# A two-layer mixer block: one projection moved ahead of the recurrence's end, four turns before its inverse, tails by banks, attention turns

## The chip, the core and the metric

The kernel runs on one core of one Trainium2 chip. The time is the device time of one execution in microseconds (us); of several executions the median is given.

## The reference

Two layers of three sublayers on x (256 rows by 1024): a gated feed-forward (width 2816), a mixer and a second feed-forward, each with an RMS norm ahead of it and one behind it. All is fp32.

```python
x = x + 0.5 * rms(ffn1(rms(x, pre)), post)
x = x + rms(mixer(rms(x, pre)), post)
x = x + 0.5 * rms(ffn2(rms(x, pre)), post)

def mixer(h):
    z_dsa, z_rwkv, z_diff, z_gate = split(h @ w_in)
    y_a = top-k attention (4 heads of 128, index scores choose 64 keys)
    y_b = rwkv recurrence (8 heads of 64): S = S * w + (S @ -kk) b + v k;  y = S @ r
    y_c = differential attention (4 heads, softmax 1 minus lam * softmax 2), rms
    proj = [y_a @ w_branch[0], y_b @ w_branch[1], y_c @ w_branch[2]]
    return (sum over n of sigmoid(z_gate[n]) * proj[n]) @ w_out
```

## The kernel before

**Wide products.** Every fp32 product is made of three fast ones: `split_to` writes hi = cast(src) on ScalarE (`wh`, `h`, `yh`) and lo = src - hi on VectorE (`wl`, `hl`, `yl`); `mm3` (L226) adds hi x lo, lo x hi and hi x hi in PSUM. A weight tile is brought by a DMA of SP's queue (`raw`), split, and used by the two row blocks t = 0, 1 of 128 rows. These wide matmuls (L229 to L235, L310) are most of TensorE's work.

**The steps.** `run_skew` (L238) runs a list of steps, each a load with split and a product for each t. The first `head` steps and the last `tail` steps are run with all of t = 0 ahead of all of t = 1, so that the norm of t = 0 runs under the products of t = 1. The tails are the last EXTRA = 7 steps of ffn1, ffn2 and the mixer. A step of 1024 output columns has two banks of PSUM of 512 each. After each step `tick` gives one turn to every small job that is open.

**The small jobs** are Python generators, and each `yield` is a turn in which a step's wide matmuls can stand. In the mixer they are `dsa` (the first attention), `rwkv_in`, `rwkv_solve` and `rwkv` (the recurrence) and `diff` (differential attention; `lm` is its softmax, `nmd` the negative maximum, `smd` the sum, `dpt` the transposed weights, `yt` its result). They run beside the products of the mixer's input columns, which end with the gate columns (`gate_steps`) and the branch projections (`proj_steps`). `drain` runs the jobs given to it until they are at their end. A tile framework puts the instructions of each engine into an order by priority and by what they wait for; `behind` keeps one behind another.

**The recurrence's inverse.** `rwkv_solve` (L996) inverts unit lower triangular matrices: first blocks of 16 by substitution on VectorE (X), which go out to device memory and back in other layouts (zs and xs, L1017 to L1024), then three levels of doubling. From zs come four matrices Z (L1032), from xs two matrices T (L1036). A level multiplies Z with `up` to W (L1063) and W with T. `zc` is a copy of Z that is transposed into the next T. After it `rwkv` (R, U, `bk`, `mb`, S) ends in y_b (`yc` and `yb` in the trace).

**The norms.** `rstd` (L323): two sums of squares on ScalarE (one per half row), an add on VectorE (L332), a power -1/2 on GpSimd (L333). `post_norm` (L384) then makes xn = ps * r * g and x = x + factor * xn for each half, and calls `pre_norm` of the next sublayer, whose xn is transposed on TensorE by the `rest` put in `later`, one row block at a time. At the end of the kernel `post_norm` writes the result out.

Of the kernel before, what the change touches and what calls it, by code (L numbers as in the profile page):

```python
# [8 lines left out]
F32 = mybir.dt.float32  # L9
F32R = mybir.dt.float32r  # L10
I32 = mybir.dt.int32
AF = mybir.ActivationFunctionType
# [27 lines left out]
class Block:  # L40
# [197 lines left out]
    def run_skew(self, steps, head=0, tail=0):  # L238

        n = len(steps)  # L240
        order = [(t, i) for t in range(2) for i in range(head)]
        order += [(t, i) for i in range(head, n - tail) for t in range(2)]
        order += [(t, i) for t in range(2) for i in range(n - tail, n)]
        held = {}
        for j, (t, i) in enumerate(order):
            if self.later and (head and j == head - 1 or tail and j == len(order) - 1):
                self.later.pop(0)()
            if t == 0:
                wait = RING <= i < head or i >= n - tail
                held[i] = steps[i][0](self.extra if wait else self.ring)  # L250
            steps[i][1](t, held[i])
            self.tick()

    def steps_b(self, rows, n, ksteps, xk, psum, done=None):
# [5 lines left out]
        def mk(k0):  # L260
# [6 lines left out]

            def go(t, w):
                if k0 == 0:
                    ps[t] = [psum() for _ in range(nb)]  # L270
                for kk in range(per):
                    xh, xl = xk(k0 + kk, t)
                    for b in range(nb):
                        c0, c1 = b * 512, min(n, b * 512 + 512)
                        self.mm3(ps[t][b][:, :c1 - c0], xh, xl, w[0][:, kk, c0:c1], w[1][:, kk, c0:c1],
                                 k0 + kk == 0, k0 + kk == ksteps - 1, False)
                if k0 + per == ksteps and done is not None:
                    done(t, ps[t])
# [44 lines left out]
    def rstd(self, parts, width):  # L323
# [7 lines left out]
        r = self.st.tile([128, 1], F32, name="rstd")  # L331
        nc.vector.tensor_scalar(r, ss[:, 0:1], ss[:, 1:2], EPS, op0=OP.add, op1=OP.add)  # L332
        nc.gpsimd.tensor_tensor(r, r, self.mhalf[:, 0:1], op=OP.pow)  # L333
# [50 lines left out]
    def post_norm(self, t, ps, g, factor):  # L384
        nc = self.nc
        with self.pn():
            r = self.rstd(ps, D)
            for h in range(2):
                s = slice(h * 512, h * 512 + 512)
                y = self.junk.tile([128, 512], F32, name="xn")  # L390
                nc.vector.scalar_tensor_tensor(y, ps[h], r, g[:, s], op0=OP.mult, op1=OP.mult)
                nc.vector.scalar_tensor_tensor(self.x[t][:, s], y, factor, self.x[t][:, s], op0=OP.mult, op1=OP.add)
                if not self.phases:
                    nc.sync.dma_start(self.out[0, t * 128:t * 128 + 128, s], self.x[t][:, s])
# [99 lines left out]
    def mixer(self, l, ctx):  # L494
# [89 lines left out]
        diff = self.start(self.diff(st, vd))  # L584
        for n, h in ((1, 0), (1, 1), (0, 0), (0, 1), (2, 1)):
            self.run_skew(gate_steps(n, h))
        self.drain(rwkv)
        c1.__exit__(None, None, None)
        self.gp = self.pool(ctx, "gp", side="right")

        def pieces(y):
            return lambda k, t: tuple(p[k // 2][:, k % 2, t * 128:t * 128 + 128] for p in y)

        yb = self.new_y(self.gp)
        with self.p1():
            for i in range(2):
                self.split_to(yb[0][i], yb[1][i], st["yb"][:, 2 * i:2 * i + 2, :])

        def proj_steps(n, y, prev=None, keep=False, last=False, acc=acc):
# [20 lines left out]
            return out  # L620

        with self.p1(), self.behind(self.exp):
            for n in range(3):
                for (m, _, _), g in gates.items():
                    if m == n:
                        nc.scalar.activation(g, g, AF.Sigmoid)
        self.run_skew(proj_steps(0, st["ya"]))
        self.run_skew(proj_steps(1, yb, prev=0, keep=True))
# [111 lines left out]
    def diff(self, st, vd):  # L740
# [10 lines left out]
        for t in range(2):  # L751
# [5 lines left out]
            for h2 in range(2):  # L757
# [13 lines left out]
                for j in range(2):  # L771
                    p0, p1 = lm[:, j, :], lm[:, 2 + j, :]
                    nc.vector.tensor_scalar(p1, p1, rs[:, 2 + j:3 + j], lam, op0=OP.mult, op1=OP.mult)
                    nc.vector.scalar_tensor_tensor(p0, p0, rs[:, j:j + 1], p1, op0=OP.mult, op1=OP.subtract)
                for _ in range(LAG):
                    yield
# [20 lines left out]
            for h in range(4):  # L797
                nc.vector.scalar_tensor_tensor(yt[:, h, :], ps[:, h, :], ss[:, h:h + 1], self.sub,
                                               op0=OP.mult, op1=OP.mult)
            yts.append(yt)  # L800
        for _ in range(2 * LAG):
            yield
# [193 lines left out]
    def rwkv_solve(self, Ls, strip):  # L996
# [42 lines left out]


        for i, mask in enumerate(self.lev):
# [4 lines left out]
            for g in range(2):  # L1046
# [222 lines left out]
```

## Time and the profile before

| what | before |
| --- | --- |
| median of 3 executions | 1435.26 us (1435.07 to 1437.74) |
| the profiled execution | 1437.46 us |
| its span | 1435.8 us |
| mean granted TensorE clock | 0.996 of full speed |
| TensorE, matmuls | 1399.8 us, 97% of the span |
| TensorE, weight loads (beside matmuls) | 1203.1 us, 84% |
| VectorE | 1012.3 us, 71% |
| ScalarE | 713.2 us, 50% |
| GpSimd | 77.5 us, 5% |

The profile is of the one execution whose own time stands in the second line; the span runs from its first to its last instruction. A share of busy time is a mean over the whole span; the rows further down show single stretches. Full clock is 1.00, and idle time printed in brackets behind a row is that of its engine just before it, with what ended it.

### The profile page before, as it was taken

What the parts mean: (1) busy time and instruction counts of PE and PEld (TensorE: products, weight loads), DVE (VectorE), ACT (ScalarE), POOL (GpSimd) and SP (SyncE); (2) the same over time, 40 slices, a digit from 0 to 9 for tenths busy, and PEclk for the clock granted to TensorE, in tenths of its full rate; (3) what the DMA queues carried; (4) which work ended last, traced back from release to release, by engine and by line L of the source; (5) the groups of instructions that cost most, each with busy time, mean ns of one, the idle gap of its engine ahead of it and who ended that gap; (6) DMA issues with size and microseconds to landing.
All of it is one profiled execution on the core that took longest, in us unless ns stands there. A gap on an engine that the chain in (4) does not pass through costs nothing.

```text
span 1435.8 us, 20311 instructions
## 1 busy us (share of the span) xinstructions
PE 1399.8 (97%) x8077; PEld 1203.1 (84%) x8077; DVE 1012.3 (71%) x1496; ACT 713.2 (50%) x1090; POOL 77.5 (5%) x92
## 2 busy tenths in 40 slices
PE   8999999999899999999999999999999999999997
PEld 5888879999688878888888888799887888788886
DVE  5777564988666877776567764659977668768753
ACT  5444454656463554444454444555545635544442
POOL 1000010121100000000000000100300000000000
PEclk9999999999999999999999999999999999999999
DMA  6665665455332564665646656554443326555653
GB/s 220 189 192 194 216 223 186 122 175 152 102 118 89 184 211 148 194 200 200 225 147 189 192 201 237 174 180 147 147 136 101 135 86 226 173 175 178 215 182 114
DMA packets 176407, 246.91 MB, mean 172 GB/s; under 512 B 17908, under 2 KB 128440, under 8 KB 176312
## 3 DMA queue, kind: packets, MB, share of 16 engines
q1 hardware_dynamic: 176312, 245.62, 52.6%
q8 instruction: 63, 1.03, 0.3%
q14 instruction: 32, 0.26, 0.1%
HBM read 241.80 MB, written 3.80 MB: 171 GB/s over the span
## 4 chain that ended last, share of the span: by engine, by line
PE 79%; DVE 9%; DMA 6%; ACT 3%; issue 2%; POOL 0%; SPq 0%; DVEq 0%; POOLq 0%; ACTq 0%
PE ps L310 28%; PE ps L233 11%; PE ps L235 11%; PE ps L234 11%; PE ps L193 7%; DVE wl L224 4%; PE ps L229 3%; PE ps L230 3%; PE ps L231 3%; ACT wh L224 2%; DMA raw<-in_w_in_dram 1%; DMA raw<-in_w_out_dram 1%; PE ps L196 1%; DMA zs<-d 1%; DMA raw<-in_ffn_w_gate_dram 1%
## 5 line engine op out<-in xcount | busy, mean ns | idle before, releaser
L224 DVE TENSOR_TENSOR wl<-raw,wh 128x1024 fp32r<-128x1024 f32 x438 | 531.8, 1222 | 240.4 <-ACT wh L224 239.2
L224 ACT CAST wh<-raw 128x1024 fp32r<-128x1024 f32 x438 | 452.9, 1045 | 453.3 <-PE ps L310 183.4
L310 PE MATMUL ps<-h,wh 128*128 128x512 f32 x1152 | 392.5, 393 | 0.0
L310 PE MATMUL ps<-h,wl 128*128 128x256 f32 x1152 | 300.2, 281 | 0.0
L310 PEld LDWEIGHTS ps<-h,wh 128*128 128x128 f32 x1152 | 206.1, 188 | 37.1
L310 PEld LDWEIGHTS ps<-h,wl 128*128 128x128 f32 x1152 | 216.9, 188 | 12.4
L233 PE MATMUL ps<-wh,h 128*128 128x512 f32 x384 | 160.0, 417 | 2.2 <-DVE h L224 1.9
L229 PE MATMUL ps<-h,wh 128*128 128x256 f32 (+1 forms) x560 | 158.6, 283 | 0.0
L230 PE MATMUL ps<-h,wh 128*128 128x256 f32 (+1 forms) x560 | 156.8, 280 | 0.0
L235 PE MATMUL ps<-wl,h 128*128 128x512 f32 x384 | 153.1, 399 | 2.8 <-DVE wl L224 2.8
L231 PE MATMUL ps<-h,wl 128*128 128x256 f32 (+1 forms) x560 | 155.7, 278 | 0.0
L234 PE MATMUL ps<-wh,h 128*128 128x512 f32 x384 | 152.2, 396 | 0.0
L233 PE MATMUL ps<-wh,gl 128*128 128x512 f32 x352 | 137.3, 390 | 0.0
L235 PE MATMUL ps<-wl,gh 128*128 128x512 f32 x352 | 137.0, 389 | 0.0
L234 PE MATMUL ps<-wh,gh 128*128 128x512 f32 x352 | 136.9, 389 | 0.0
L229 PEld LDWEIGHTS ps<-h,wh 128*128 128x128 f32 (+1 forms) x560 | 104.8, 187 | 2.0 <-issue 1.3
L230 PEld LDWEIGHTS ps<-h,wh 128*128 128x128 f32 (+1 forms) x560 | 104.9, 187 | 0.3
L231 PEld LDWEIGHTS ps<-h,wl 128*128 128x128 f32 (+1 forms) x560 | 104.7, 187 | 0.1
L235 PEld LDWEIGHTS ps<-wl,h 128*128 128x128 f32 x384 | 72.7, 189 | 22.6 <-DVE wl L224 5.6
L233 PEld LDWEIGHTS ps<-wh,h 128*128 128x128 f32 x384 | 72.5, 189 | 20.2 <-issue 3.3
L234 PEld LDWEIGHTS ps<-wh,h 128*128 128x128 f32 x384 | 72.8, 190 | 13.4
L235 PEld LDWEIGHTS ps<-wl,gh 128*128 128x128 f32 x352 | 66.1, 188 | 13.9
(272 smaller groups left out, 1715.0 us busy)
## 6 DMA issues: line engine op xcount, KB each, us to landing
raw<-in_w_in_dram SPq DMA_DIRECT2D x66, 1024.0 KB, 5.1
raw<-in_ffn_w_up_dram SPq DMA_DIRECT2D x44, 1024.0 KB, 5.4
raw<-in_ffn_w_down_dram SPq DMA_DIRECT2D x44, 1024.0 KB, 4.9
raw<-in_ffn_w_gate_dram SPq DMA_DIRECT2D x43, 1024.0 KB, 5.4
raw<-in_w_branch_dram SPq DMA_DIRECT2D x12, 1024.0 KB, 4.9
raw<-in_w_out_dram SPq DMA_DIRECT2D x8, 1024.0 KB, 5.6
gpre<-in_ffn_norm_pre_dram SPq DMA_DIRECT2D x4, 512.0 KB, 5.2
gpost<-in_ffn_norm_post_dram SPq DMA_DIRECT2D x4, 512.0 KB, 6.3
```

Source lines behind the costliest of these rows:

```text
L193: self.small = self.nc.tensor.matmul(*a, **k)
L196: self.small = self.nc.tensor.transpose(*a, **k)
L224: return self.nc.scalar.copy(hi, src), self.nc.vector.tensor_sub(lo, src, hi.bitcast(F32))
L229: mm(ps, wh, xl, start=first, stop=False)
L230: mm(ps, wh, xh, start=False, stop=False)
L231: self.last = mm(ps, wl, xh, start=False, stop=last)
L233: mm(ps, xl, wh, start=first, stop=False)
L234: mm(ps, xh, wh, start=False, stop=False)
L235: self.last = mm(ps, xh, wl, start=False, stop=last)
L310: self.last = mm(*a, start=k == i == 0, stop=k == 7 and i == 1)
```

## The change

1. The tails of `run_skew` go by banks: for each t first bank 0 of all seven steps, then bank 1. `later` is popped one step earlier.
2. The add of `rstd` moves from VectorE to GpSimd. In `post_norm` the product ps * factor * g is made for both halves ahead, and only x + xn * r follows the root.
3. In the mixer the sigmoids of the first branch's gates (`open_gates(0)`) and the projection of the first branch (`proj_steps(0)`) go in front of `drain(rwkv)`.
4. `diff` has 2 * LAG = 4 turns, not 2, ahead of lm's transposes, and one more turn for each t at its end.
5. `rwkv_solve` has four turns, not one, ahead of Z and T; the T matrices are made on VectorE, in the third and fourth of the four rounds, not on GpSimd in the first two; the first level has one turn more.

```diff
     def run_skew(self, steps, head=0, tail=0):
-        order += [(t, i) for t in range(2) for i in range(n - tail, n)]
+        order += [(t, i, b) for t in range(2) for b in range(2) for i in range(n - tail, n)]
...
-            if self.later and (head and j == head - 1 or tail and j == len(order) - 1):
+            if self.later and (head and j == head - 1 or tail and j == len(order) - 2):
...
-            if t == 0:
+            if i not in held:
...
-                    for b in range(nb):
+                    for b in range(nb) if only is None else (only,):
...
     def rstd(self, parts, width):
-        nc.vector.tensor_scalar(r, ss[:, 0:1], ss[:, 1:2], EPS, op0=OP.add, op1=OP.add)
+        nc.gpsimd.tensor_scalar(r, ss[:, 0:1], ss[:, 1:2], EPS, op0=OP.add, op1=OP.add)
...
     def post_norm(self, t, ps, g, factor):
+            ys = []
             for h in range(2):
+                y = self.junk.tile([128, 512], F32, name="xn")
+                nc.vector.scalar_tensor_tensor(y, ps[h], factor, g[:, h * 512:h * 512 + 512], op0=OP.mult, op1=OP.mult)
+                ys.append(y)
+            for h, y in enumerate(ys):
                 s = slice(h * 512, h * 512 + 512)
-                y = self.junk.tile([128, 512], F32, name="xn")
-                nc.vector.scalar_tensor_tensor(y, ps[h], r, g[:, s], op0=OP.mult, op1=OP.mult)
-                nc.vector.scalar_tensor_tensor(self.x[t][:, s], y, factor, self.x[t][:, s], op0=OP.mult, op1=OP.add)
+                nc.vector.scalar_tensor_tensor(self.x[t][:, s], y, r, self.x[t][:, s], op0=OP.mult, op1=OP.add)
...
-        for n, h in ((1, 0), (1, 1), (0, 0), (0, 1), (2, 1)):
-            self.run_skew(gate_steps(n, h))
-        self.drain(rwkv)
...
+        for n, h in ((1, 0), (1, 1), (0, 0), (0, 1), (2, 1)):
+            self.run_skew(gate_steps(n, h))
+            if (n, h) == (0, 1):
+                with self.p1():
+                    open_gates(0)
+        self.run_skew(proj_steps(0, st["ya"]))
+        self.drain(rwkv)
...
-            for n in range(3):
-                for (m, _, _), g in gates.items():
-                    if m == n:
-                        nc.scalar.activation(g, g, AF.Sigmoid)
-        self.run_skew(proj_steps(0, st["ya"]))
+            open_gates(1, 2)
...
-                for _ in range(LAG):
+                for _ in range(2 * LAG):
                     yield
                 for s in range(t + 1):
...
             yts.append(yt)
+            yield
...
         Zs, Ts = [], []
-        yield
+        for _ in range(2 * LAG):
+            yield
...
-            if q < 2:
+            if q > 1:
                 Ts.append(self.ep.tile([128, 4, 128], F32, name="T", tag="s"))
-                nc.gpsimd.tensor_tensor(Ts[q].rearrange("p v (g x) -> p v g x", x=16),
-                                        xs[:, 4 * q:4 * q + 4, None, :].to_broadcast([128, 4, 8, 16]), even, op=OP.mult)
+                nc.vector.tensor_tensor(Ts[-1].rearrange("p v (g x) -> p v g x", x=16),
+                                        xs[:, 4 * q - 8:4 * q - 4, None, :].to_broadcast([128, 4, 8, 16]), even, op=OP.mult)
             yield
...
+            if not i:
+                yield
```

What stands where on TensorE and VectorE, in the inverse of layer 0, and on ScalarE in the recurrence behind it:

TensorE before, from the last wide matmul ahead of the first W,T to the transposes of lm. Ahead of these rows stand dk,dq (the attention's scores), six wide matmuls, Z,up, six, Z,up and six:

```order
L235 MATMUL ps<-wl,h 128x512
L193 MATMUL ps<-W,T 128x128 x4
L233 MATMUL ps<-wh,h 128x512
L234 MATMUL ps<-wh,h 128x512
L235 MATMUL ps<-wl,h 128x512
L196 MATMUL ps<-ident,lm 128x128
```

TensorE in the change, to the same transposes. Ahead of these rows stand dk,dq, 24 wide matmuls, Z,up and three:

```order
L233 MATMUL ps<-wh,h 128x512
L234 MATMUL ps<-wh,h 128x512
L235 MATMUL ps<-wl,h 128x512
L193 MATMUL ps<-Z,up_3196 128x128 x4
L196 MATMUL ps<-ident,lm 128x128 x2
L233 MATMUL ps<-wh,h 128x512
```

The transposes of lm stood behind W,T, and now stand right behind the second group of Z,up. From dk,dq to the transposes of zc are 30 wide matmuls before and 54 now; from the recurrence's last U,mb group to the last transposes of yc are 30 in both.

VectorE before, from the three Z that wait for zs (nmd, lm and smd are the softmax's; wl is a weight split):

```order
L1032 TENSOR_TENSOR Z<-zs,blk_1732 128x512 x3
L224 TENSOR_TENSOR wl<-raw,wh 128x1024
L1032 TENSOR_TENSOR Z<-zs,blk_1732 128x512
L767 SCALAR_TENSOR_TENSOR lm<-ps,cmS 128x256
L224 TENSOR_TENSOR wl<-raw,wh 128x1024
L767 SCALAR_TENSOR_TENSOR lm<-ps,cmS 128x256
L653 TENSOR_REDUCE nmd<-lm 128x4
L1063 TENSOR_TENSOR W<-ps,blk_1732 128x512 x2
L224 TENSOR_TENSOR wl<-raw,wh 128x1024
L656 RECIPROCAL smd<-smd 128x4
L773 TENSOR_SCALAR lm<-lm,smd,lam 128x128 x2
L774 SCALAR_TENSOR_TENSOR lm<-lm,smd 128x128 x2
```

VectorE in the change, from the same Z:

```order
L1043 TENSOR_TENSOR Z<-zs,blk_1732 128x512 x3
L224 TENSOR_TENSOR wl<-raw,wh 128x1024
L1047 TENSOR_TENSOR T<-xs,even 128x512
L1043 TENSOR_TENSOR Z<-zs,blk_1732 128x512
L224 TENSOR_TENSOR wl<-raw,wh 128x1024
L776 SCALAR_TENSOR_TENSOR lm<-ps,cmS 128x256 x2
L1047 TENSOR_TENSOR T<-xs,even 128x512
L662 TENSOR_REDUCE nmd<-lm 128x4
L224 TENSOR_TENSOR wl<-raw,wh 128x1024
L665 RECIPROCAL smd<-smd 128x4
L782 TENSOR_SCALAR lm<-lm,smd,lam 128x128 x2
L783 SCALAR_TENSOR_TENSOR lm<-lm,smd 128x128 x2
```

Both T stand on VectorE now, and W comes behind the last lm; both lm and nmd are still behind the three Z.

ScalarE before, where the sigmoids of the gates start (R, U are the recurrence's, g the gates, lm the attention's exponentials):

```order
L655 ACTIVATE lm,smd<-lm,nmd 128x256 x4
L626 ACT_TABLE_LOAD
L626 ACTIVATE g_3765<-g_3765 128x512
L224 CAST wh<-raw 128x1024
L626 ACTIVATE g_3789<-g_3789 128x512
L626 ACTIVATE g_3765<-g_3765 128x512
L1136 COPY R<-ps 128x256
L782 COPY dpt_3866<-ps 128x256
L626 ACTIVATE g_3789<-g_3789 128x512
L626 ACTIVATE g<-g 128x512
L224 CAST wh<-raw 128x1024
```

ScalarE in the change, from the first R copy:

```order
L1149 COPY R<-ps 128x256
L618 ACT_TABLE_LOAD
L618 ACTIVATE g_4128<-g_4128 128x512
L224 CAST wh<-raw 128x1024
L538 COPY g_4128<-ps 128x512
L664 ACT_TABLE_LOAD
L664 ACTIVATE lm,smd<-lm,nmd 128x256 x2
L224 CAST wh<-raw 128x1024
L664 ACTIVATE lm,smd<-lm,nmd 128x256 x2
L1149 COPY R<-ps 128x256
L1158 COPY U<-ps 128x256
L618 ACT_TABLE_LOAD
```

A sigmoid stands between the first R copy and four exponentials, with a table load on each side, and the second R copy stands behind them; a third table load stands behind the first U copy.

## Rows read from the trace of the kernel before

**Rows 1.** the page's part 1: busy us (share of span) and instructions

```profile
PE 1399.8 (97%) x8077; PEld 1203.1 (84%) x8077; DVE 1012.3 (71%) x1496; ACT 713.2 (50%) x1090; POOL 77.5 (5%) x92
```

**Rows 2.** windows, layer 0's inverse: busy us by engine, PEclk, DMA, GB/s

```profile
375.10:378.40 3.30, 3.23 (x13) 2.80 (x13) 1.73 (x4) 2.03 (x4) 0.00 (x0) 0.57 0.95 313
```

**Rows 3.** timeline of TensorE in both inverses: start, duration (us), instruction [idle before <-releaser]

```profile
361.43 0.39 PE L234 MATMUL ps<-wh,h 128*128 128x512 f32 x1
361.66 0.39 PE L235 MATMUL ps<-wl,h 128*128 128x512 f32 x1
...
364.75 0.68 PE L193 MATMUL ps<-Z,up 128*128 128x128 f32 x4 [0.98 <-DVE Z L1032]
...
368.17 0.68 PE L193 MATMUL ps<-Z,up 128*128 128x128 f32 x4 [0.90 <-DVE Z L1032]
...
371.29 1.13 PE L193 MATMUL ps<-W,T 128*128 128x128 f32 x8 [1.04 <-DVE W L1063]
...
375.17 0.30 PE L196 MATMUL ps<-ident,lm 128*128 128x128 f32 x1 [2.05 <-DVE lm L774]
...
380.81 0.60 PE L196 MATMUL ps<-ident,zc 128*128 128x128 f32 x4
...
1085.09 0.30 PE L196 MATMUL ps<-ident,lm 128*128 128x128 f32 x1 [2.05 <-DVE lm L774]
```

**Rows 4.** timeline of VectorE in layer 0's inverse, the same columns

```profile
362.25 4.04 DVE L1032 TENSOR_TENSOR Z<-zs,blk 128x512 f32<-128x512 f32 x3 [4.67 <-DMA zs<-d]
366.21 1.22 DVE L224 TENSOR_TENSOR wl<-raw,wh 128x1024 fp32r<-128x1024 f32 x1
367.35 0.68 DVE L1032 TENSOR_TENSOR Z<-zs,blk 128x512 f32<-128x512 f32 x1
367.95 0.41 DVE L767 SCALAR_TENSOR_TENSOR lm<-ps,cmS 128x256 f32<-128x256 f32 x1
...
369.86 0.69 DVE L653 TENSOR_REDUCE nmd<-lm 128x4 f32<-128x512 f32 x1
...
374.68 0.61 DVE L774 SCALAR_TENSOR_TENSOR lm<-lm,smd 128x128 f32<-128x128 f32 x2
```

**Rows 5.** timeline of GpSimd in the same stretch

```profile
362.65 3.09 POOL L1036 TENSOR_TENSOR T<-xs,even 128x512 f32<-128x512 f32 x2 [31.59 <-DMA xs<-d]
```

**Rows 6.** timeline of ScalarE where the gates' sigmoids begin, layer 0

```profile
414.43 0.51 ACT L655 ACTIVATE lm<-lm,nmd 128x256 f32<-128x256 f32 x1 [3.96 <-DVE nmd L653]
...
416.52 1.28 ACT L626 ACT_TABLE_LOAD   x1
417.82 0.63 ACT L626 ACTIVATE g<-g 128x512 f32<-128x512 f32 x1
418.36 1.03 ACT L224 CAST wh<-raw 128x1024 fp32r<-128x1024 f32 x1
```

**Rows 7.** timeline of TensorE: dk,dq in front of yt, a small group later

```profile
395.13 1.13 PE L193 MATMUL ps<-dk,dq 64*128 64x256 f32 x4 [0.66 <-DVE yt L798]
...
417.76 1.00 PE L193 MATMUL ps<-vt,lk 128*128 128x64 f32 x8
```

**Rows 8.** timeline of VectorE in the last norm of the kernel

```profile
1430.21 1.41 DVE L391 SCALAR_TENSOR_TENSOR xn<-ps,rstd,gpost 128x512 f32<-128x512 f32 x2 [0.73 <-POOL rstd L333]
1431.53 1.28 DVE L392 SCALAR_TENSOR_TENSOR xr<-xn,xr 128x512 f32<-128x512 f32 x2
```

**Rows 9.** timeline of GpSimd: a norm's pow without and with a split beside it

```profile
526.25 0.56 POOL L333 TENSOR_TENSOR rstd<-rstd,mhalf 128x1 f32<-128x1 f32 x1 [57.35 <-DVE rstd L332]
...
904.01 1.39 POOL L333 TENSOR_TENSOR rstd<-rstd,mhalf 128x1 f32<-128x1 f32 x1 [5.16 <-DVE rstd L332]
```

**Rows 10.** timeline of VectorE: the add of the norm behind layer 0's mixer

```profile
525.96 0.21 DVE L332 TENSOR_SCALAR rstd<-ss 128x1 f32<-128x1 f32 x1
```

**Rows 11.** timeline of TensorE: xn's transposes behind the mixers of both layers

```profile
532.23 0.63 PE L362 MATMUL ps<-ident,xn 128*128 128x128 f32 x4 [1.84 <-DVE xn L353]
...
1240.99 0.63 PE L362 MATMUL ps<-ident,xn 128*128 128x128 f32 x4 [1.36 <-DVE xn L353]
```

More of the change, by code (lines that the diff above doesn't have):

```diff
@@ L240, in run_skew @@
         n = len(steps)
-        order = [(t, i) for t in range(2) for i in range(head)]
-        order += [(t, i) for i in range(head, n - tail) for t in range(2)]
-        order += [(t, i) for t in range(2) for i in range(n - tail, n)]
+        order = [(t, i, None) for t in range(2) for i in range(head)]
+        order += [(t, i, None) for i in range(head, n - tail) for t in range(2)]
+        order += [(t, i, b) for t in range(2) for b in range(2) for i in range(n - tail, n)]
         held = {}
-        for j, (t, i) in enumerate(order):
-            if self.later and (head and j == head - 1 or tail and j == len(order) - 1):
+        for j, (t, i, b) in enumerate(order):
+            if self.later and (head and j == head - 1 or tail and j == len(order) - 2):
                 self.later.pop(0)()
-            if t == 0:
+            if i not in held:
                 wait = RING <= i < head or i >= n - tail
                 held[i] = steps[i][0](self.extra if wait else self.ring)
-            steps[i][1](t, held[i])
+            steps[i][1](t, held[i], b)
             self.tick()
@@ L266, in ld, with go @@
                 return self.split(raws[0][:, o:o + per, :], per, n, pool)
-            def go(t, w):
+            def go(t, w, only):
                 if k0 == 0:
@@ L276, in go @@
                                  k0 + kk == 0, k0 + kk == ksteps - 1, False)
-                if k0 + per == ksteps and done is not None:
+                if k0 + per == ksteps and done is not None and only in (None, nb - 1):
                     done(t, ps[t])
@@ L584, in mixer @@
         diff = self.start(self.diff(st, vd))
-        for n, h in ((1, 0), (1, 1), (0, 0), (0, 1), (2, 1)):
-            self.run_skew(gate_steps(n, h))
-        self.drain(rwkv)
-        c1.__exit__(None, None, None)
-        self.gp = self.pool(ctx, "gp", side="right")
         def pieces(y):
             return lambda k, t: tuple(p[k // 2][:, k % 2, t * 128:t * 128 + 128] for p in y)
[L594 to L597, printed above, removed]
         def proj_steps(n, y, prev=None, keep=False, last=False, acc=acc):
@@ L620, in proj_steps, with open_gates @@
             return out
-        with self.p1(), self.behind(self.exp):
-            for n in range(3):
-                for (m, _, _), g in gates.items():
-                    if m == n:
-                        nc.scalar.activation(g, g, AF.Sigmoid)
-        self.run_skew(proj_steps(0, st["ya"]))
+        def open_gates(*ns):
+            for (n, _, _), g in gates.items():
+                if n in ns:
+                    nc.scalar.activation(g, g, AF.Sigmoid)
+        for n, h in ((1, 0), (1, 1), (0, 0), (0, 1), (2, 1)):
[5 more added lines that the diff above has]
+        self.drain(rwkv)
+        c1.__exit__(None, None, None)
+        self.gp = self.pool(ctx, "gp", side="right")
+        yb = self.new_y(self.gp)
+        with self.p1():
+            for i in range(2):
+                self.split_to(yb[0][i], yb[1][i], st["yb"][:, 2 * i:2 * i + 2, :])
+        with self.p1(), self.behind(self.exp):
+            open_gates(1, 2)
         self.run_skew(proj_steps(1, yb, prev=0, keep=True))
```

## The prediction

> **What bounds the kernel now.** I read the page's busy shares first. The matmul rows of TensorE fill 97% of the span, so it is the bound, and no other engine's busy time is worth anything until it makes TensorE wait [rows 1]. The second view was TensorE's own rows with the idle time printed behind them. The reader is to see that nearly all of the idle time stands in short bursts at a few places, and the change touches most of them: the inverse of the recurrence (once in each layer), the first rows behind it, and the joints where one sublayer's norm stands between two runs of matmuls. The third view was the wide windows, for the clock: behind the inverse's longest wait TensorE goes on at a granted clock of 0.57, most of that stretch at the lower of its two levels, 1.2 GHz (full speed is 1.00) [rows 2]. So that wait costs more than its own length.
>
> The inverse of layer 0, row by row. TensorE starts its wide matmuls (pace 361.66 - 361.43 = 0.23 us) and then waits 0.98, 0.90 and 1.04 us for VectorE's Z and W and 2.05 us for lm, the attention's softmax, whose transposes stand in front of the next matmuls [rows 3]. From 361.43 to the transposes of zc at 380.81 it takes 19.4 us. The four waits are 5.0 us; the half-speed stretch loses 3.3 x 0.43 = 1.4 us; some 1.3 us go into shorter gaps and into starting again after each. I count 7.7 us lost, an estimate from these rows. On VectorE's side one sees why [rows 4]: three Z take 4.04 us, 1.35 each, where the fourth, alone, takes 0.68. In that time GpSimd makes the two T, 3.09 us [rows 5]. All else on VectorE (split weights, lm, nmd) is in order behind the first Z, which waits 4.67 us for its DMA.
>
> **The inverse, as changed.** Four turns in place of one before the matrices put 18 more wide matmuls between dk,dq and the first Z,up, and the extra turn in the first level 6 behind it: 24 x 0.23 = 5.5 us of work that is taken from later, not added. T goes to VectorE, behind Z. VectorE's chain from the same landing, 362.25, by its rows [rows 4]: three Z at 0.68, 2.0; a split weight 1.14 from start to start; T 0.6; Z 0.6; a split weight 1.14; lm twice 0.35; T 0.6: nmd starts near 369.0 instead of 369.86. Then nmd 0.69, four exponentials at about 0.4 (the tile of twice the width takes 0.51 [rows 6]), then reciprocal and lm, 1.2, and hand-overs of 0.3: TensorE has the first lm at 373.0, not at 375.2, because W x2 and a late split weight no longer stand between. TensorE gets there at 361.4 + 5.3 + two Z,up groups of 0.9 + six wide of 1.4 = 369.9, and waits 3.1 us, in one piece. So 7.7 lost becomes 3.1 plus what the clock does. After a wait of 2.05 us, with others ahead of it, the clock fell; one of 3.1 us may do the same, 1.4. If it falls, the gain is 3.2, if not, 4.6; some 0.3 of the short gaps will stay. I take the fall, as the nearest row shows it, so 2.9 a layer: **5.8**, and the same for the second layer, whose lm waits 2.05 us too [rows 3]. The bounds are 0 (the landing comes later by as much as the filler covers) and 7.7 a layer.
>
> The T moved off GpSimd costs VectorE 1.2 us in that chain and gives back 2.0 at Z, so it is a gain by itself. Without the fillers it would be 0.8.
>
> **The yt wait.** TensorE waits 0.66 us for yt in front of dk,dq in layer 0 [rows 7], about 0.9 with the restart, and the second layer repeats it. One more turn per row block moves it. Bounds 0 and 1.8; I take half, **0.9**.
>
> **The first projection and the gates.** No matmul is added. The recurrence's end keeps its distance from the fillers: 30 wide matmuls stand before the last yc transposes as before. The cost is ScalarE's: the sigmoids of the first gate go in front of an exponential of the attention, so two more table loads a layer, 1.28 us each [rows 6]. Queued behind the first are one sigmoid 0.63, a weight cast 1.03, a gate copy, the load back, four exponentials of 0.5, a cast, and then the second R copy, which TensorE wants: 0.4 + 1.28 + 0.63 + 1.03 + 0.6 + 1.28 + 2.0 + 1.0 = 8.2, with R's own copy 8.6 us. TensorE has 29 wide matmuls and three small groups of about 0.9 (one row shows 1.00, and such rows overlap the next by 0.1 to 0.2 [rows 7]) in that time, 6.7 + 2.7 = 9.4 us. So 0.8 us of slack; then the next load, sigmoid and cast stand before the second U, 3 us against 3 us of matmuls. Bounds 0 and 2.6 a layer (both loads in full); I take 0.5: **-1.0** for two.
>
> The Trainium skill, ScalarE: Activation LUTs, section What ACT_TABLE_LOAD costs, says that a switch takes 1283 ns plus a drain of some 1380 ns, 2.66 us in all. The first number agrees with the row. The drain doesn't show: the load ends at 417.80 and the sigmoid starts at 417.82, and the exponentials before it end just as it starts. By that section the R copy would be some 2.8 us later, and TensorE would wait about 2 us for it and 1.4 us for U: 7 us for both layers, and 1432.4 for the whole, an estimate from the skill's figure. The sum goes by the row.
>
> **Norms and joints.** In the post norm the product with the gain goes in front of the root. At the end the two xn start at 1430.21 and the two x only at 1431.53 [rows 8]: 1.32 us leave the chain, here and at the joints, whose rows have the same lengths. The add becomes a GpSimd instruction that the trace doesn't have; the nearest row is GpSimd's pow on the same tile, 0.56 [rows 9], against 0.21 for VectorE's add [rows 10]. From the add's start to the pow's are 0.29 us there, so 0.27 more for each norm if add and pow queue back to back, and 0.5 for a joint, which has two. The tail by banks lets the first half's squares (0.6) run under the second half's matmuls. At mix-to-ffn2 of layer 0 the net is 1.3 - 0.5 + 0.6 = 1.4, out of 1.84 us of idle [rows 11]. The same in layer 1, whose idle is 1.36 [rows 11]: together **2.8**. At ffn1-to-mix of layer 1 a weight cast sits between the squares and takes part of it away: **0.6**. At the end, where every us counts fully, it is 1.3 - 0.3 = **1.0** (the last matmul is of the second half either way). At the start nothing is saved, and a memset of GpSimd now stands between add and pow: **-0.4**, an estimate from 0.27 and its like. Elsewhere the norms lie under the other row block's matmuls.
>
> The bank order wants the last weights earlier: a pass over one bank of seven steps takes 7 x 3 x 0.23 = 4.8 us instead of 9.7, so the last split could be late by up to that; but the order fills the pass with bank 1's matmuls where weights come late. Bounds 0 and 4 in all; I take **-0.85**.
>
> **Sum.** 5.8 + 0.9 - 1.0 + 2.8 + 0.6 + 1.0 - 0.4 - 0.85 = 8.85 us less. The profiled execution took 1437.46 (span 1435.8), 2.2 above the median of the three runs, 1435.26; so 1428.6 against the profiled execution, **1426.4** against the median. A measurement of this kernel can tell about 0.2%, 2.9 us, from no change.
>
> **Rivals.**
> (a) The clock stays up behind the single wait, or lm comes earlier, so TensorE hardly waits: the inverse gives 4.3 a layer, and yt its whole 1.8. For it: the work ahead is dense, where before there were four waits in a row. 1426.4 - 3.7 = 1422.7.
> (b) The wait only moves. VectorE is still head of line behind the first Z, and the DMA of zs still sets it; with weights wanted sooner the transfer may land later, since it shares the queue. Then the filler is eaten by the lm wait, the inverse gives nothing, and 1426.4 + 5.8 = 1432.2 is left.
> (c) The table switches hold R and U, in full on each: 1426.4 + 4.2 = 1430.6. The rows speak against it by 0.8 us of slack.
> (d) Slower: GpSimd's two norm instructions are held by VectorE's weight splits. In the joint of layer 1 a pow beside a split takes 1.39 instead of 0.56 [rows 9]. If add and pow are both held, a norm's root takes 2.8 instead of 0.85; the three joints of two norms lose 3 x (3.9 - 1.3) - 1.2 for the banks = 6.6, the end 0.6 and the start 0.9, together 8.1 where the forecast has a gain of 4.0: 1426.4 + 12.1 = 1438.5. It passes the time of before once three quarters of these instructions are held; of the two pow rows here one is.
> The Trainium skill, SBUF — State Buffer, section Who interferes with whom, states the rule behind this: a VectorE instruction with two SBUF inputs and a GpSimd one that reads SBUF block each other for a whole instruction. The 1.35 us Z beside T and the 1.39 us pow agree.
> (e) The last weights come late in every tail: 1426.4 + 3.2 = 1429.6.
>
> **Chances.** The forecast 0.42 (own range 1424 to 1429), (a) 0.20, (b) 0.15, (c) and (e) together 0.14, (d) 0.09. The range reaches from a little under (a), 1419.5, to past (b), 1434. Half of (b) and a part of (c) lie within 0.2% of before: same 0.13; slower is (d) with a little for (b), 0.09; faster 0.78.
>
> **What would show it.** Right: the three Z near 0.68 each; one idle of about 3.1 us at ident,lm and no Z or W waits ahead of it; the second R copy at most 0.5 us before its matmul's wait ends; the transposes of xn idling under 0.7 us at the two mixer ends; xr straight behind the pow at the end. Wrong: an lm idle over 5 us, a granted clock near 0.57 over more than 3.5 us, an idle before R,Z or U,bk over 1 us, GpSimd roots over 2 us at the joints, or waits for wl in the tails.

## The result, and the profile after

The changed kernel takes 1426.73 us (median of five, 1422.83 to 1430.6) against 1435.26 (median of five, 1433.5 to 1440.2); the ratio is 0.9931, interval 0.9904 to 0.9959, so between 0.4 and 1.0% faster. The profiled execution took 1425.25 us, span 1423.5, 12.2 less than that of before: two single executions, that of before 2.2 us above its median and that of the change 1.5 below. The stages below are compared by these two traces, so their gains add up to some 12 us and not to the 8.5 between the medians.

The page's part 1 of the changed kernel, which answers to [rows 1]:

```profile
PE 1394.4 (98%) x8077; PEld 1198.8 (84%) x8077; DVE 1006.0 (71%) x1476; ACT 718.1 (50%) x1094; POOL 84.9 (6%) x112
```

TensorE runs the same 8077 matmuls with 5.4 us less of busy time, at a mean granted clock of 0.998 instead of 0.996, so a part of the gain is in how fast they ran, and the rest is idle time.

**The inverse.** TensorE's timeline, three rows of layer 0 and one of layer 1, beside [rows 3]:

```profile
368.66 1.05 PE L193 MATMUL ps<-Z,up 128*128 128x128 f32 x8
...
372.43 0.50 PE L196 MATMUL ps<-ident,lm 128*128 128x128 f32 x2 [2.71 <-DVE lm L783]
...
380.94 0.60 PE L196 MATMUL ps<-ident,zc 128*128 128x128 f32 x4
...
1073.00 0.50 PE L196 MATMUL ps<-ident,lm 128*128 128x128 f32 x2 [3.81 <-DVE lm L783]
```

The four waits of before are one: 2.71 us at lm's transposes in layer 0 and 3.81 in layer 1. The windows behind them, one of layer 0 and two of layer 1 (the column ahead of the DMA share is the granted clock), beside [rows 2]:

```profile
372.40:375.70 3.30, 3.27 (x20) 2.45 (x21) 3.18 (x6) 2.08 (x4) 0.00 (x0) 1.00 0.78 290
...
1072.90:1076.20 3.30, 3.20 (x16) 2.18 (x16) 2.55 (x4) 2.02 (x4) 0.00 (x0) 0.73 0.79 294
...
1076.20:1079.50 3.30, 3.30 (x17) 2.86 (x16) 2.58 (x4) 0.66 (x4) 0.00 (x0) 0.75 0.15 24
```

In layer 0 the clock stays at 1.00, in layer 1 it falls to 0.73 and 0.75. VectorE's timeline in layer 0 says where the time came from, beside [rows 4]:

```profile
362.25 1.90 DVE L1043 TENSOR_TENSOR Z<-zs,blk 128x512 f32<-128x512 f32 x3 [4.66 <-DMA zs<-d]
...
365.20 0.68 DVE L1047 TENSOR_TENSOR T<-xs,even 128x512 f32<-128x512 f32 x1
...
368.80 0.68 DVE L662 TENSOR_REDUCE nmd<-lm 128x4 f32<-128x512 f32 x1
...
371.93 0.61 DVE L783 SCALAR_TENSOR_TENSOR lm<-lm,smd 128x128 f32<-128x128 f32 x2
```

zs lands at 362.25 as before, and the three Z now take 1.90 us instead of 4.04. The last lm stands at 371.93, where it was at 374.68.

For the stages I add up by how much each matmul starts later than the start of the one before it plus that one's pace (0.23 us for 512 columns, 0.11 for 256 or 128); this sum is called the loss. Between the first dk,dq and the first transposes of zc the loss was 9.3 us in layer 0 and 10.7 in layer 1, and is 4.2 and 6.8: 9.0 us less. (Some 1.5 us of it are changes from one kind of matmul to another and stay in every run.) From there to the end of the recurrence's last R,Z group it was 10.5 and 10.4 and is 11.0 in both: 1.1 us more. From yt's last transposes to xn's it was 3.4 and 2.3, and is 1.0 and 3.1.

One trace is one execution. Three of the runs below leave the inverse as the change has it (the projection behind the drain again, the norms as before, the tails by steps), and there the same stretch loses 5.2 and 4.6, 5.5 and 3.8, 3.9 and 3.6 us, with waits of 2.2 to 3.1 us at lm's transposes. So against the one trace of before the inverse's gain lies between 9.0 and 12.5 us, and the 6.8 of layer 1 above is the largest loss of the eight.

**Behind the inverse.** The wait for yt, 0.66 us in each layer [rows 7], is gone; in its place stands one for lk, in TensorE's timeline:

```profile
444.65 0.70 PE L193 MATMUL ps<-ar,bk 64*128 64x256 f32 x2 [1.05 <-DVE lk L1134]
```

VectorE ahead of it waits for GpSimd's pow of the attention and of the recurrence, since yt now falls into the recurrence's end:

```profile
442.59 0.35 DVE L807 SCALAR_TENSOR_TENSOR yt<-ps,dss,sub 128x128 f32<-128x128 f32 x1 [0.90 <-POOL dss L804]
...
443.57 0.42 DVE L1198 TENSOR_TENSOR yc<-yc,var 128x256 f32<-128x256 f32 x1 [0.63 <-POOL var L1197]
...
443.91 1.28 DVE L1134 TENSOR_TENSOR lk<-ps,mT 128x512 f32<-128x512 f32 x2
```

The table switches on ScalarE, beside [rows 6]:

```profile
417.15 0.37 ACT L1149 COPY R<-ps 128x256 f32<-128x256 f32 x1 [0.25 <-PE ps L193]
...
417.54 1.28 ACT L618 ACT_TABLE_LOAD   x1
...
418.83 0.63 ACT L618 ACTIVATE g<-g 128x512 f32<-128x512 f32 x1
...
421.12 1.28 ACT L664 ACT_TABLE_LOAD   x1
...
426.10 0.35 ACT L1149 COPY R<-ps 128x256 f32<-128x256 f32 x1
...
426.73 1.28 ACT L618 ACT_TABLE_LOAD   x1
```

From the first R copy to the second are 8.95 us. TensorE's second R,Z group and its second U,bk group:

```profile
426.69 1.00 PE L193 MATMUL ps<-R,Z 128*128 128x64 f32 x8
...
430.55 0.38 PE L193 MATMUL ps<-U,bk 128*128 128x128 f32 x2
```

Neither has idle time ahead of it. What was costed with 1.0 us for two layers is within the overlap.

**The joints.** TensorE's transposes of xn behind both mixers, beside [rows 11], and between them a wait in the tail of layer 1's mixer:

```profile
525.08 1.29 PE L363 MATMUL ps<-ident,xn 128*128 128x128 f32 x8 [0.27 <-DVE xn L354]
...
1215.84 0.50 PE L233 MATMUL ps<-wh,ml 128*128 128x512 f32 x1 [1.87 <-DVE ml L224]
...
1229.27 1.29 PE L363 MATMUL ps<-ident,xn 128*128 128x128 f32 x8 [0.22 <-DVE xn L354]
```

1.84 and 1.36 us of idle are 0.27 and 0.22. In layer 1 a wait of 1.87 for ml, in the tail of the mixer, takes the gain back. ScalarE there:

```profile
1211.74 2.00 ACT L224 CAST wh<-raw 128x1024 fp32r<-128x1024 f32 x2 [5.05 <-DMA raw<-in_w_out_dram]
...
1213.65 1.06 ACT L224 CAST mh<-ps 128x512 fp32r<-128x512 f32 x2
```

It waits 5.05 us for a transfer of w_out, and mh stands in order behind that split. At the end of the kernel GpSimd and VectorE, beside [rows 8 to 10]:

```profile
1418.22 0.30 POOL L333 TENSOR_SCALAR rstd<-ss 128x1 f32<-128x1 f32 x1 [8.58 <-ACT junk L331]
...
1418.61 0.56 POOL L334 TENSOR_TENSOR rstd<-rstd,mhalf 128x1 f32<-128x1 f32 x1
```

```profile
1419.20 1.41 DVE L396 SCALAR_TENSOR_TENSOR xr<-xn,rstd,xr 128x512 f32<-128x512 f32 x2 [0.35 <-POOL rstd L334]
```

The add takes 0.30 us on GpSimd; x follows the pow at once, and the stretch from the last matmul's start to the end of the span is 6.6 us instead of 7.7.

### The profile page after: what moved, and what is told of

Its sections match the earlier page's. It is cut to its first block, busy times and chain, and to the rows that moved or that the text cites. A ratio compares the mean times of both kernels' runs of the same rounds, so it can differ in the third digit from the quotient of the medians.

```text
span 1423.5 us, 20349 instructions
## 1 busy us (share of the span) xinstructions
PE 1394.4 (98%) x8077; PEld 1198.8 (84%) x8077; DVE 1006.0 (71%) x1476; ACT 718.1 (50%) x1094; POOL 84.9 (6%) x112
```

## The experiments

Each run's median is compared with that of before, 1435.4 to 1435.7 in the same runs. The loss between dk,dq and zc is given for layer 0 and layer 1.

**One turn ahead of Z.** The changed kernel without the four turns:

```diff
-        for _ in range(2 * LAG):
+        for _ in range(1):
             yield
         for q in range(4):
```

> The changed kernel with one turn instead of four ahead of Z and T; all else stays. Theory A (the turns are filler under the wait for zs and lm, and carry most of the inverse's gain): TensorE's waits between dk,dq and the transposes of zc come back to 7 to 8 us lost in each layer from 4.2 and 6.8 now, the first of them for Z; median 1430 to 1434. Theory B (the gain comes from T leaving GpSimd, Z at 0.63 instead of 1.35): the loss stays within 1 us of the changed kernel's, median 1426 to 1428.

Measured: 1420.14 us, ratio 0.989 (0.9867 to 0.9912); loss 2.6 and 3.7. Both theories missed: without the turns the kernel is faster, by 6.6 us between the medians. (The two traces differ by 3.3 us of span. The rest lies in the executions that were not profiled; over all of them the mean granted clock has a median of 0.997 in the changed kernel and 0.999 here.) TensorE's timeline in layer 0, two Z,up rows and lm's transposes:

```profile
363.52 1.29 PE L193 MATMUL ps<-Z,up 128*128 128x128 f32 x8 [0.31 <-DVE Z L1043]
...
367.07 0.68 PE L193 MATMUL ps<-Z,up 128*128 128x128 f32 x4 [0.42 <-DVE Z L1043]
...
373.52 0.44 PE L196 MATMUL ps<-ident,lm 128*128 128x128 f32 x2
```

The waits for Z are 0.31 and 0.42 us (1.35 and 0.42 in layer 1), and lm's transposes, which now stand behind both W,T, wait for nothing in either layer. The fillers had been put where there was little left to fill, and they had moved W,T, the work that covers the softmax, behind lm's transposes. Of the gain 0.8 us a layer come back between zc and the last R,Z group.

**T on GpSimd again**, four turns kept:

```diff
-            if q > 1:
+            if q < 2:
-                nc.vector.tensor_tensor(Ts[-1]..., xs[:, 4 * q - 8:4 * q - 4, ...
+                nc.gpsimd.tensor_tensor(Ts[-1]..., xs[:, 4 * q:4 * q + 4, ...
```

> The changed kernel with the two T made on GpSimd beside the first Z, as before; four turns stay. Theory A: three Z take 4.0 us again (2.1 more), VectorE is spared 1.2 us of T in the chain, so lm comes 0.9 us later: the wait at lm's transposes is 3.6 instead of 2.7 in layer 0 and 4.9 instead of 4.0 in layer 1; with the clock falling in both layers 2 to 4 us in all, median 1428.5 to 1431. Theory B: most of the inverse's gain is gone, median 1433 or more.

Measured: 1429.6 us, ratio 0.9955 (0.9934 to 0.9976); loss 7.5 and 8.6. The median is in theory A's range. Lm waits 0.7 us longer in layer 0 but only 0.1 in layer 1 (3.92 against 3.81; the expectation's 4.0 stands in no row); the rest is the clock, which fell in both. Lm's transposes in layer 0, and the window behind them:

```profile
374.79 0.66 PE L196 MATMUL ps<-ident,lm 128*128 128x128 f32 x2 [3.43 <-DVE lm L783]
```

```profile
375.00:378.30 3.30, 3.30 (x10) 2.27 (x11) 2.26 (x3) 1.29 (x3) 0.00 (x0) 0.50 0.72 276
```

**Z behind the softmax's maximum.** Six turns, and an order on VectorE:

```diff
+                self.scored = self.nmd
...
-        for _ in range(2 * LAG):
+        for _ in range(6):
...
-            with self.behind(self.attended):
+            with self.behind(self.attended, self.scored):
                 nc.vector.tensor_tensor(Zs[q]...
```

> The changed kernel with six turns ahead of Z, and Z ordered behind the maximum (nmd) of the attention's softmax on VectorE, so that the softmax no longer stands behind the wait for zs. Theory A (what is left of the inverse's loss is lm standing in order behind Z): the 2.7 and 4.0 us waits at lm's transposes go, no wait over 1 us takes their place, the granted clock stays at 1.00 in both layers; 6 to 8 us less than the changed kernel, median 1419 to 1421. Rival (the wait moves to Z, to the weight splits, or to the recurrence's end, which now comes two turns later): at least half of it comes back there, median 1424 to 1428.

Measured: 1418.29 us, ratio 0.9876 (0.9851 to 0.9901), the lowest median of all, though its interval holds the ratios of four other runs; loss 1.9 and 1.9. Lm's transposes in layer 0, and on VectorE nmd ahead of Z:

```profile
374.14 0.30 PE L196 MATMUL ps<-ident,lm 128*128 128x128 f32 x1 [0.43 <-DVE lm L784]
```

```profile
367.80 0.69 DVE L662 TENSOR_REDUCE nmd<-lm 128x4 f32<-128x512 f32 x1
...
368.40 1.28 DVE L1044 TENSOR_TENSOR Z<-zs,blk 128x512 f32<-128x512 f32 x2
```

The wait is 0.43 us. Of the gain 1.2 us a layer come back at the last transposes of yc, as the rival had it in part (the stretch from yc's last two groups of transposes to yt's loses 1.6 us where the changed kernel loses 0.4).

**The projection behind the drain again:**

```diff
...
-                    open_gates(0)
-        self.run_skew(proj_steps(0, st["ya"]))
         self.drain(rwkv)
...
-            open_gates(1, 2)
+            open_gates(0, 1, 2)
+        self.run_skew(proj_steps(0, st["ya"]))
```

> The changed kernel with the first projection and all sigmoids behind the drain again, as before; the four turns stay. Theory A (the table switches cost about 0.5 us a layer, and 30 wide matmuls ahead of the last transposes are cover enough for four or five turns of six): two table loads a layer fewer, the waits of 1.05 us at lk in front of ar,bk unchanged or gone, no wait over 1 us at the recurrence's end; within 3 us of the changed kernel, 1424 to 1428. Rival (the recurrence, five turns later, is no longer covered without the projection): TensorE idles 3 to 6 us a layer between the last U,mb and the transposes of yc, median 1432 or more.

Measured: 1429.06 us, ratio 0.9953 (0.9936 to 0.997), 1.1 us over what theory A allowed and well under the rival. The yc to yt stretch loses 1.3 us instead of 0.4 in each layer, and lk waits 1.37 us instead of 1.05. So the projection ahead covers about 1 us a layer of the recurrence's end, and the table loads cost less than that.

**T alone.** The kernel before with only the T matrices on VectorE (the same lines as above, the other way):

> The kernel before with one edit: the two T made on VectorE in the third and fourth round, not on GpSimd. The last runs say that four turns ahead of Z cost time and that with one turn nearly nothing is lost between dk,dq and zc; open is whether T alone does that. Theory C (T beside Z was the inverse's loss: it made Z 2.1 us later, and lm, W and the clock followed): the loss between dk,dq and zc falls from 9.3 and 10.7 to 3 to 5 us in each layer, Z three times in 1.9 us, clock 1.00; 5 to 6 us a layer, median 1423 to 1427. Theory D (T and the attention's two more turns ahead of lm's transposes are both needed): lm's transposes still wait 1 to 2 us, the loss stays at 5 to 8 us, median 1428 to 1432.

Measured: 1429.64 us, ratio 0.9962 (0.9941 to 0.9982); loss 5.6 and 6.3, from 9.3 and 10.7. That is 3.7 and 4.4 us by one edit, the larger part. The waits in layer 0 add up to 3.2 us (0.31, 0.42, 0.83 and 1.63) where before had 5.3 (0.34, 0.98, 0.90, 1.04 and 2.05); in layer 1 to 3.9 instead of 5.4. That is 2.1 and 1.5 us, against 2.15 that the three Z take less (1.89, not 4.04). Most of the rest is the clock: it stays at 1.00 in both layers here, and before it fell to 0.57 once in layer 0, and in layer 1 to 0.59 and 0.57. What is still lost is as theory D had it, since W,T and lm still wait:

```profile
370.12 1.16 PE L193 MATMUL ps<-W,T 128*128 128x128 f32 x8 [0.83 <-DVE W L1063]
...
373.61 0.30 PE L196 MATMUL ps<-ident,lm 128*128 128x128 f32 x1 [1.63 <-DVE lm L774]
```

**Two turns ahead of lm's transposes**, one ahead of Z:

```diff
     def diff(self, st, vd):
-                for _ in range(2 * LAG):
+                for _ in range(LAG):
                     yield
                 for s in range(t + 1):
```

> The changed kernel with one turn ahead of Z and two, not four, ahead of lm's transposes. Theory C: T alone is what counts, so this is within 2 us of the run with one turn and four ahead of lm, median 1419 to 1423. Theory D: lm's transposes stand 13 wide matmuls behind Z,up without the first W,T and wait 1 to 2 us in each layer: median 1423 to 1426.

Measured: 1430.7 us, ratio 0.9961 (0.9944 to 0.9977); loss 7.1 and 7.9. Worse than both expectations, 10.6 us over the run with one turn and four ahead of lm. By the loss, 4.5 and 4.2 us, the attention's two more turns are worth as much as T: a wait of 2.68 us (2.71 in layer 1) comes back, and the clock falls behind it. Lm's transposes and the window behind:

```profile
372.87 0.30 PE L196 MATMUL ps<-ident,lm 128*128 128x128 f32 x1 [2.68 <-DVE lm L783]
```

```profile
373.00:376.30 3.30, 3.30 (x19) 2.92 (x18) 1.53 (x2) 0.69 (x2) 0.00 (x0) 0.51 0.74 284
```

**The turns alone.** The kernel before with only the inverse's turns:

```diff
-        yield
+        for _ in range(2 * LAG):
+            yield
         for q in range(4):
...
+            if not i:
+                yield
```

> The kernel before with the inverse's turns alone: four ahead of Z and T, one more in the first level; T stays on GpSimd, two turns ahead of lm's transposes, all else as before. Theory A, as the prediction had it (the turns are filler and carry the gain): the loss between dk,dq and zc falls to 4 to 6 us in each layer, median 1427 to 1430. Theory C (the turns take W,T away from in front of lm's transposes and fill nothing): one long wait of 5 to 7 us at lm's transposes, the loss stays at 8 to 11 us, the clock falls in both layers, median 1433 to 1438.

Measured: 1442.94 us, ratio 1.0048 (1.0033 to 1.0064): slower than before, and worse than C expected. The one wait is there, and Z beside T as before:

```profile
373.11 0.45 PE L196 MATMUL ps<-ident,lm 128*128 128x128 f32 x1 [5.28 <-DVE lm L774]
```

```profile
361.80 4.11 DVE L1033 TENSOR_TENSOR Z<-zs,blk 128x512 f32<-128x512 f32 x3 [4.63 <-DMA zs<-d]
```

The loss in this stretch is 9.1 and 9.4, 1.5 us less than before in both layers together. What the trace shows to be slower lies behind it: from yc's last two groups of transposes to yt's the loss is 1.3 us instead of 0.4 in each layer, where the recurrence ends four turns later and the projection still stands behind it. The profiled execution of this run, 1438.84 us, lies 4.1 us below the run's median. Its mean granted clock is 0.995, and the median over the twelve executions is 0.992. Three thousandths of 1440 us are 4.3 us, an estimate that would cover the difference; where in these executions the clock fell stands in no trace.

**All turns of the inverse undone:** one ahead of Z, none more in the first level (the edit is the two above, the other way, in the changed kernel).

> The changed kernel with all turns of the inverse as before (one ahead of Z, none more in the first level); T on VectorE and the other parts of the change stay. Theory C: no turn of the inverse is worth anything; lm's transposes now stand behind those of zc and wait for nothing; within 2 us of the run with one turn, median 1419 to 1422. Rival (the first level's extra turn covers W on VectorE): a wait of 0.5 to 1 us at W,T or zc in each layer, median 1422 to 1424.

Measured: 1419.76 us, ratio 0.9883 (0.9863 to 0.9903); loss 3.5 and 4.2, with a 0.83 us wait at W,T in each layer as the rival had it, and between zc and the last R,Z group 1.6 us less in each layer than the run with one turn. The time is theory C's. So the change gains without any turn in the inverse. T on VectorE with the attention's turns alone, without the projection, the norms and the banks, was not run.

**Six turns, no extra turn in the first level.**

> The run with six turns and Z behind nmd, without the extra turn in the first level, so that the recurrence ends six wide matmuls earlier. Its waits of 0.6 and 0.8 us behind the last transposes of yc get shorter by up to 0.6 in each layer, unless W is late without the turn; median 1416.5 to 1419. If W is late (0.5 us or more at W,T), nothing is gained: 1418 to 1420.

Measured: 1419.33 us, ratio 0.9886 (0.9866 to 0.9906). Missed: the wait behind yc is not shorter (the stretch loses 1.7 us instead of 1.6), and nothing is gained; W isn't late either (loss 1.9 and 1.5).

**One turn, projection behind the drain** (the two edits above together):

> The run with one turn ahead of Z, with the first projection and all sigmoids behind the drain as before. Theory E (the projection was moved to cover the turns and is worth nothing without them; the two table loads cost under 0.5 us a layer): within 2 us of that run, median 1418 to 1422. Rival (the projection covers the recurrence's end also with one turn): waits of 0.8 us or more behind the transposes of yc in each layer, median 1422 to 1425.

Measured: 1421.95 us, ratio 0.9899 (0.9881 to 0.9917), 1.8 us over the run with one turn. The time is inside theory E's range, but the wait of 0.93 us ahead of the last yc transposes is the rival's: the projection is worth about 1 us a layer with one turn, too. The medians can't tell 1.8 us apart.

**The norms as before**, tail by banks kept:

```diff
-        nc.gpsimd.tensor_scalar(r, ss[:, 0:1], ss[:, 1:2], EPS, op0=OP.add, op1=OP.add)
+        nc.vector.tensor_scalar(r, ss[:, 0:1], ss[:, 1:2], EPS, op0=OP.add, op1=OP.add)
...
-                nc.vector.scalar_tensor_tensor(y, ps[h], factor, g[:, h * 512:h * 512 + 512], op0=OP.mult, op1=OP.mult)
...
-                nc.vector.scalar_tensor_tensor(self.x[t][:, s], y, r, self.x[t][:, s], op0=OP.mult, op1=OP.add)
+                nc.vector.scalar_tensor_tensor(y, ps[h], r, g[:, s], op0=OP.mult, op1=OP.mult)
+                nc.vector.scalar_tensor_tensor(self.x[t][:, s], y, factor, self.x[t][:, s], op0=OP.mult, op1=OP.add)
```

> The changed kernel with the norm's add on VectorE and the post norm's two products behind the root, as before; the tail by banks stays. Theory A (the product moved ahead of the root takes 1.3 us out of every joint that is in sight): 1.0 us more at the end, waits of 0.8 to 1.5 us at the transposes of xn behind both mixers and ffn1 of layer 1, 3 to 5 us in all, median 1429 to 1432. Rival (the tail by banks alone covers the joints): only the 1.0 us at the end, median 1427 to 1428.

Measured: 1428.77 us, ratio 0.9957 (0.9943 to 0.9971), between the two expectations; waits at xn behind both mixers (1.67 and 0.87), none at ffn1 of layer 1. The 2.0 us over the changed kernel are too few for the medians to tell; 1.1 of them stand at the end of the kernel in the trace.

**The tails by steps**, norms of the change kept:

```diff
-        order += [(t, i, b) for t in range(2) for b in range(2) for i in range(n - tail, n)]
+        order += [(t, i, None) for t in range(2) for i in range(n - tail, n)]
...
-            if self.later and (head and j == head - 1 or tail and j == len(order) - 2):
+            if self.later and (head and j == head - 1 or tail and j == len(order) - 1):
```

> The changed kernel with the tails by steps again, each with both banks. Theory A (the banks give the first half's squares 0.6 us of start and cost up to 0.85 us in late weights): waits of about 0.6 us at the transposes of xn behind the mixers and ffn1 of layer 1, and the waits for ml in the mixers' tails (0.4 to 2.0 us) gone or smaller; within 2 us, median 1425 to 1428. Rival (the banks carry the joints: with the last products of the first half 4.8 us ahead its norm has begun long before): 1 to 2 us of wait at each of three joints, median 1430 or more.

Measured: 1427.12 us, ratio 0.9944 (0.9923 to 0.9965): theory A's time, 0.4 us from the changed kernel, so the banks bring nothing that the medians show; but at layer 0's mixer it has the rival's wait, three times what theory A had there. The transposes of xn behind layer 0's mixer, first with the norms as before, then with the tails by steps:

```profile
529.13 1.29 PE L363 MATMUL ps<-ident,xn 128*128 128x128 f32 x8 [1.67 <-DVE xn L354]
```

```profile
527.22 1.29 PE L363 MATMUL ps<-ident,xn 128*128 128x128 f32 x8 [1.90 <-DVE xn L354]
```

In layer 0 either edit alone leaves nearly all of the 1.84 us of before, and both together leave 0.27. The other eight runs with both edits have 0 to 0.5 us there in both layers, but for one wait of 1.42 (layer 0, the projection behind the drain).

At ffn1 of layer 1 the trace of before has a wait of 1.96 us, and both runs have none. That does not show the edits at work: T alone, with the norms and tails of before, waits 0.19 us there, and the turns alone, with the same, not at all. First before, then T alone:

```profile
906.24 0.99 PE L362 MATMUL ps<-ident,xn 128*128 128x128 f32 x5 [1.96 <-DVE xn L353]
```

```profile
902.42 1.32 PE L362 MATMUL ps<-ident,xn 128*128 128x128 f32 x8 [0.19 <-DVE xn L353]
```

The end stretch is 7.7 us with the norms as before and 6.7 with the tails by steps: that 1.0 us is the norms'.

## Why the prediction was right, and which step was not

The time was right, 1426.4 against 1426.73, and that close by luck in part. Between the two profiled executions 8.85 us were forecast and 12.2 came. The largest term was too small, others were too large, and the gain of the largest came from another cause than the one given.

**The inverse** was put at 5.8 us, and the two traces show 9.0. The landing of zs, Z at 0.63, and one wait of 2.7 and 3.8 at lm's transposes came as worked out (3.1). The step that failed is the attribution: "Four turns in place of one" as filler, and of T, "Without the fillers it would be 0.8". T alone gave 3.7 and 4.4 us; the turns alone gave a slower kernel; and within the change the turns cost 1.6 and 3.2 us of loss in these two traces (with the other runs, 3.6 to 6.8 a layer with four turns against 2.5 to 3.7 with one). I had priced T by the time that it takes from and gives back to VectorE, 2.0 less 1.2. In fact the 2.1 us of Z were late for Z,up, W, W,T and lm one after the other, without that the waits came down by 2.1 and 1.5 us, and the granted clock, which had fallen behind them, stayed up. And I had costed the attention's two further turns at nothing, where a run without them loses 4.2 to 4.5 us a layer more. The first is visible in the rows that I showed: the releasers of the four waits are Z, Z, W and lm [rows 3]; the second came out of the run alone.

**yt and the tables.** +0.9 and -1.0 were forecast; the wait for yt went, 0.66 in each layer, and a wait of 1.05 for lk came. The stretch is 1.1 us worse in sum, and that wait is the step that the forecast lacks. The tables took nothing that shows at R,Z or U,bk. The page ScalarE: Activation LUTs of the Trainium skill, section What ACT_TABLE_LOAD costs, adds a drain of some 1380 ns to each switch. In these rows none shows: a load starts 0.02 us after the work ahead of it has ended, and the work behind it 0.01 us after the load.

**The joints and the end.** 2.8 for the mixers' ends: the waits at xn came down by 1.57 and 1.14 us, 2.7 in all, but the wait for ml took 1.87 back in layer 1. It is in some traces and not in others, with tails by banks (none in the run with T on GpSimd again) and by steps (0.49 us in layer 0 of before, 1.86 there in the turns alone), and stands behind a transfer that lands late; what makes it late wasn't tried. So the tails' -0.85 can't be told from this wait. 0.6 at ffn1 of layer 1: a wait of 1.96 is gone, which the runs do not show to be the change's. 1.0 at the end: 1.1, in every run with the new norms. At the start the first transposes of xn wait 0.48 us before and 1.17 after, and 0.55 to 2.01 in the other runs, so the -0.4 is not shown either way.

**Rivals.** (a) came half true, since the clock held in one layer; over the four traces with this inverse it held in five layers of eight. (b) did not come in the change, and (c) did not: R and U wait for nothing. Of (e) one tail came late. (d) was half the mechanism: GpSimd's two norm instructions are held once, not twice. GpSimd's groups, where [rows 9] had 1.39 for a held pow:

```profile
L333 POOL TENSOR_SCALAR rstd<-ss 128x1 f32<-128x1 f32 x24 | 19.0, 792 | 852.7 <-ACT junk L331 852.7
...
L334 POOL TENSOR_TENSOR rstd<-rstd,mhalf 128x1 f32<-128x1 f32 x24 | 13.5, 563 | 1.9
```

The pow is never held any more, 0.56 in each of 24; the add is held instead, in 10 of 24 instances 0.9 to 1.7 us. Before, the 24 pow had a mean of 842 ns with an add of 210 ahead on VectorE; now both together are 1355, some 0.3 more for each norm. At the mixers' ends the post norm's add of the first row block is held (1.33 and 0.93); its pre norm's and the last one of the kernel are not (0.30).

## What to carry to other kernels

When one engine's late start shows as four waits with four names, price the first cause by all of them, and by the clock behind them, before adding filler. Then check what extra turns move away from in front of the next wait: here they moved W,T away from in front of lm. Two edits may cover one wait only together, as the norms and banks do behind layer 0's mixer, so each alone says little. And a wait that one trace has and another lacks is not yet the work of an edit: look for it in a run that leaves that edit out.

## What the runs showed of the hardware that was not expected

The granted clock does not follow the length of one wait alone. It stayed at 1.00 behind a wait of 2.71 us (layer 0 of the change) and fell to 0.51 behind one of 2.68 (two turns ahead of lm's transposes); it fell to 0.50 behind 3.43 and to 0.73 behind 3.81. Short waits ahead don't decide it either. The run with the projection behind the drain has the changed kernel's inverse, and between dk,dq and lm's transposes TensorE waits nowhere else in either layer. Behind 2.33 us in layer 0 the clock was 0.53, and behind 3.14 us in layer 1 it was 1.00:

```profile
371.60:374.90 3.30, 3.27 (x10) 2.26 (x12) 2.48 (x4) 0.95 (x3) 0.00 (x0) 0.53 0.77 287
1075.70:1079.00 3.30, 3.30 (x20) 2.45 (x21) 3.18 (x6) 2.03 (x4) 0.00 (x0) 1.00 0.75 288
```

So a wait of this kind comes out either way, and what decides it the runs don't tell.

The executions of one kernel differ by the clock, too: of 23 of before the fastest took 1431.97 us at a mean granted clock of 0.999 and the slowest 1446.68 at 0.989. The changed kernel's five lie between 0.994 and 0.998 and spread over 7.8 us; the six with one turn ahead of Z, without a wait at lm, lie between 0.997 and 0.999 and spread over 3.5.
